# Hybrid encoder on one core: the prompt's attention output goes through DRAM, layer norms stand between output-projection products, w_out's low parts of the sample move to VectorE

## The chip, the cores and the metric

The kernel runs on one core of one Trainium2 chip. It is one program of 20112 instructions. The metric is the device time of one execution in microseconds; the median of three runs before the change is 1564.66 us. TensorE (PE in the profile) multiplies, VectorE (DVE), ScalarE (ACT) and GpSimd (POOL) do the elementwise work, and nearly all DMAs are issued by SyncE (SP), in the order of its queue. Each engine takes its instructions in a fixed order, and an instruction that waits holds up all behind it on its engine.

## The reference

One layer of an encoder runs on two inputs with shared weights: the prompt (512 rows) and the sample (1024 rows), both 1024 wide, all in float32.

```
h = RMSNorm(x); z = h @ w_in                       # 1024 -> 1792: q, k, v, ca, cb
a = windowed attention(q, k, v)                    # 8 heads of 64, 2 kv heads, |q - k| <= 128, bias, sink
c = silu(LayerNorm(dwconv31(ca * sigmoid(cb))))    # 512 channels, norm over channels
x = x + concat(a, c) @ w_out                       # 1024 -> 1024
h = RMSNorm(x); u = dwconv3(h @ w_up)              # 1024 -> 2 x 2816
x = x + (silu(u_gate) * u_value) @ w_down
y = RMSNorm(x)
```

## The kernel before

**Precision.** A float32 product is made of three matmuls on fp32r tiles: each operand is split into a high part, a rounded copy (ScalarE, `split`, L192), and a low part, the difference (L193, on GpSimd, or on VectorE where `dve` is set). So a weight costs one copy, one subtraction and, for a half-product of 128 x 512 with 8 blocks of rows of the weight, 24 matmuls.

**Stages.** The blocks are 128 rows: 0 to 3 are the prompt, 4 to 11 the sample. (1) The prompt's input projection (`proj` and `step`, L299 to L302), 14 chunks of 128 columns. (2) The sample's input projection, the same 14 chunks times two halves of 512 rows, 28 steps; beside it runs the generator `prompt()`: the prompt's attention (`scores`, `values`), its layer norms (`conv_norm`), its output projection (`out_half`, L726 to L728) and its second RMSNorm with transposes (`make_h2`, L776; `transposed`, L258 to L261). (3) The prompt's up-projection, 22 steps of `ffn_step`; beside it, from step 2 on, runs `sample()`: the sample's attention, the loading and splitting of w_out and two of its layer norms. (4) The sample's output projection with the other norms, and then up- and down-projection by products of blocks, up to the end.

**What sets the order.** The program text interleaves the stages by ticks: `proj` calls `tick()` three times in its 24 matmuls and `step` once more, so a step has four. A tick adds `pace["rate"]` to a counter, and for each whole unit the side generator is advanced by one `yield`. The rates are the constants of the head: RB while the prompt's attention runs, RBO from its end on, RD in the up-projection, RN after the sample's attention. In the same way each tick adds a credit for the taps of the 31-wide convolutions, a chain of VectorE instructions (L354), each of which costs 0.66: CA and CB for the prompt's, CL, CLO and CD for the sample's, which are called late. After the main loop of a stage `drain(side)` takes what is left of the side generator, with nothing interleaved. The result is the program order. From it a planner makes the order of each engine: it simulates the engines with costs of its own and lets the earliest instruction of the program go first among those that are ready. `behind` sets an instruction back by a number of places (BACK, for the prompt's and the sample's convolutions).

**Memory.** `sb` hands out fixed slots of SBUF (`h` of 2 KB for each partition, `q` of 4 KB and others); a slot that is used again waits for its last user. The concatenated operand of the output projection is in `cats[i, part]`: part 0 the attention of block i, part 1 the normed convolution, each a high and a low tile. The prompt's part 0 stays in SBUF from `values` to `out_half`; the sample's goes to DRAM (`catd`, L661) and is read back by `load_cat` (L676).

**A layer norm.** `conv_norm` loads the convolution's output from DRAM, transposes it on PE (L690), takes its statistics on VectorE (L692, L693), the power -1/2 on GpSimd (L176, L177), scales on VectorE (L696), yields YN = 2 more times, transposes back on PE (L702), and goes through ScalarE and VectorE to part 1 of `cats` (L705 to L710). For the prompt it first drains the prompt's convolutions.

**An output product.** `out_half(i, n)` makes half n of block i: 24 matmuls with three yields between, and the addition to x (L731). With the second half of a block it stores x, sums its squares (L737) and has the inverse root made on GpSimd. `make_h2` scales the four blocks by it and transposes them; the up-projection's first matmul needs the first transposes of all four.

**A bank.** The up-projection's results lie in two PSUM banks (`u`), which are free again after one ScalarE instruction (L856) and two VectorE instructions (L852) of `up_half`.

Of the kernel before, what the change touches and what calls it, by code (L numbers as in the profile page):

```python
# [36 lines left out]

RA, RB, RBO, RD, RN, RE = 1.2, 0.8, 2.5, 0.8, 0.95, 0.9  # L40


CA, CB = 0.9, 0.4
CL, CLO, CD = 0.6, 1.0, 0.6

NOFF = (4, 7)

SCB, SCD = "aapa", "aaap"


WOP, WOA, DW, DW2 = 1, 5, 2, 0
NE = 2
YN = 2
OB = "uc"
# [2 lines left out]
KEEP = 3  # L57


BACK = (200, 1500)  # L60
U0 = 2


# [82 lines left out]
def tile_hybrid_encoder(ctx: ExitStack, tc: tile.TileContext, xs, rel_bias, norm_attn_g, w_in,  # L146
# [144 lines left out]
    def drain(queue):  # L291
        while queue:
            advance(queue)
# [15 lines left out]
    qsd = [dr.tile([4, P, NH, P], F32, name=f"qsd{i}") for i in range(3)]  # L309
    vsd = dr.tile([P, 2, NKV, 4, P], F32, name="vsd")  # L310
    ksd = dr.tile([HD, NKV, 2, 1024], F32, name="ksd")
    catd = dr.tile([8, P, 2, 4 * P], F32, name="catd")
    cvd = [dr.tile([P, 4, G["T"]], F32, name=f"cvd{G['g']}") for G in GR]
    rs2 = cst.tile([P, 12], F32, name="rs2")

# [303 lines left out]
    def values(u):  # L619
        i, kv = divmod(u, 2)  # L620
        G, b = blocks[i]
        kts = window(i)
        cat = cat_of(i, 0)
        pr = units.pop(u)
        nt0 = 0 if i < 4 else 1
        ht = []

        def turn(n):
            pt = bank("attn")
            for j in range(GRP):  # L630
                nc.tensor.transpose(pt[:, j * P:(j + 1) * P], pr[j][:, 1 + n * P:1 + (n + 1) * P], ident[:])
            hi, lo = sb.tile([NT], F32R), sb.tile([NT], F32R)
            nc.scalar.copy(hi[:], pt[:])
            nc.vector.tensor_tensor(lo[:], pt[:], hi[:].bitcast(F32), op=ALU.subtract)
            ht.append((hi, lo))

        turn(0)
        yield 0.0
        turn(1)
        po = bank("attn")  # L640
        for n, k in enumerate(kts):
            yield 0.0
            hi, lo = ht[n]
            v = vt[nt0 + k // 4][kv][:, k % 4, :]
            nc.tensor.matmul(po[:], v, hi[:], start=(n == 0), stop=False)
            nc.tensor.matmul(po[:], v, lo[:], start=False, stop=(n == len(kts) - 1))
            ht[n] = hi = lo = None
            if n + 2 < len(kts):
                turn(n + 2)
        rows = slice(kv * HD, (kv + 1) * HD)  # L650
        rest = slice((1 - kv) * HD, (2 - kv) * HD)
        c, d = sb.tile([NT]), sb.tile([NT])
        nc.scalar.copy(c[rows, :], po[rest, :])
        nc.scalar.copy(cat[0][rows, :, :], po[rows, :].rearrange("p (j t) -> p j t", t=P))
        nc.vector.tensor_tensor(d[rows, :], po[rows, :], cat[0][rows, :, :].bitcast(F32).rearrange("p j t -> p (j t)"),
                                op=ALU.subtract)
        nc.gpsimd.tensor_tensor(cat[1][rows, :, :].rearrange("p j t -> p (j t)"), d[rows, :], c[rows, :], op=ALU.add)
        if kv == 1 and G["g"] == 1:
            cats.pop((i, 0))
            for L in range(2):  # L660
                nc.sync.dma_start(catd[b, :, L, :].rearrange("p (j t) -> p j t", t=P), cat[L][:].bitcast(F32))  # L661
        yield 0.0

    def attention(u0, u1, then={}):
# [8 lines left out]
    def load_cat(i):  # L673
        cats[i, 0] = (sb.tile([4, P], F32R), sb.tile([4, P], F32R))
        for L in range(2):
            nc.sync.dma_start(cats[i, 0][L][:].bitcast(F32), catd[blocks[i][1], :, L, :].rearrange("p (j t) -> p j t", t=P))  # L676

    def conv_norm(i):
        G, b = blocks[i]
        if G["g"] == 0:  # L680
            drain(convs)
        cat = cat_of(i, 1)
        cv = sb.tile([4, P])
        nc.sync.dma_start(cv[:], cvd[G["g"]][:, :, b * P:(b + 1) * P])
        if G["g"] == 1 and (i, 0) not in cats:
            load_cat(i)
        yield 0.0
        pt = bank("norm")
        for c in range(4):
            nc.tensor.transpose(pt[:, c * P:(c + 1) * P], cv[:, c, :], ident[:])  # L690
        st, mv, rs = sm(6), sm(2), sm(1)
        nc.vector.bn_stats(st[:], pt[:])  # L692
        nc.vector.bn_aggr(mv[:], st[:])  # L693
        rstd_of(mv[:, 1:2], 1.0, rs[:])
        xh = sb.tile([CCH])
        nc.vector.tensor_scalar(xh[:], pt[:], mv[:, 0:1], rs[:], op0=ALU.subtract, op1=ALU.mult)  # L696
        del pt
        for _ in range(YN):
            yield 0.0
        p2 = bank("norm")  # L700
        for c in range(4):
            nc.tensor.transpose(p2[:, c * P:(c + 1) * P], xh[:, c * P:(c + 1) * P], ident[:])  # L702
        y, t = sb.tile([4, P]), sb.tile([4, P])
        for c in range(4):
            nc.scalar.activation(y[:, c, :], p2[:, c * P:(c + 1) * P], AF.Identity,  # L705
                                 scale=lng[:, c:c + 1], bias=lnb[:, c:c + 1])
        nc.scalar.activation(t[:], y[:], AF.Tanh)
        nc.vector.scalar_tensor_tensor(t[:], t[:], 1.0, y[:], op0=ALU.add, op1=ALU.mult)
        nc.scalar.copy(cat[0][:], t[:])
        nc.vector.tensor_tensor(cat[1][:], t[:], cat[0][:].bitcast(F32), op=ALU.subtract)  # L710
        yield 0.0

    xr, x1, wo = {}, {}, {}
    x1d = [dr.tile([P, D], F32, name=f"x1d{i}") for i in range(12)]

    def out_half(i, n):
# [12 lines left out]
            if kc % 2 == 1 and kc < KC - 1:  # L729
                yield 0.0  # L730
        nc.vector.tensor_tensor(x[:, s], po[:], x[:, s], op=ALU.add)  # L731
        if n == 1:
            x1[i] = x
            nc.sync.dma_start(x1d[i][:], x[:])
            ss = sm(1)
# [46 lines left out]

    use.update(step="b", turn="a", attn="au", norm="au", out="u")

    def prompt():
        yield from attention(0, 8, {u: conv_norm(u - 4) for u in range(4, 8)})
        kt.clear(), vt.clear(), qt.clear(), bias.clear()
        pace.update(rate=RBO, late=CLO)
        for n in range(2):
            for kc in range(KC):  # L790
                if (kc, n) not in wor:
                    load_wo(kc, n)
            yield 0.0
            for kc in range(KC):
                split_wo(kc, n, kc % 2 < DW)
                if kc % 2 == 1:
                    yield 0.0
            for i in range(4):
                if n == 0 and i == 3:
                    for kc in range(WOP):  # L800
                        load_wo(kc, 1)
                yield from out_half(i, n)
            wo.clear()
        yield from make_h2(0, 0)

    seq = [(GR[0], j) for j in range(NJ)]
# [105 lines left out]
        want_up(0, half)  # L912
    want_up_raw(1, 0)
    load_bias()
    def sample():
        sink_columns()
        yield from attention(8, 24)
        kt.clear(), vt.clear(), qt.clear(), bias.clear(), score_rows.clear()
        use.update(norm="a")
        pace.update(rate=RN)  # L920
        for m in range(16 + WOA):
            if m in (10, 12):
                load_cat(m // 2 - 1)
            if m < 16:
                load_wo(m // 2, m % 2)
            if m >= WOA:
                split_wo((m - WOA) // 2, m % 2, m % 4 < DW2)
                yield 0.0
        drain(late)
        for m in range(NE):  # L930
            yield from conv_norm(4 + m)

    pace.update(rate=RD, late=CD)
    for k in range(NJ):
# [723 lines left out]
```

## Time and profile before

| | |
|---|---|
| median of 3 runs | 1564.66 us (1561.09 to 1566.85) |
| the profiled execution | 1561.29 us |
| its span, first to last instruction | 1559.5 us |
| mean granted TensorE clock | 0.990 |
| busy: TensorE, VectorE, ScalarE, GpSimd | 1505.8, 1126.9, 795.2, 709.7 us |
| moved between HBM and the core | 227.17 MB, mean 146 GB/s |

Stage 2 lies between about 109 and 366 us, the prompt's up-projection between 366 and 686 us, the sample's output projection between 686 and about 790 us. A row of a stretch of time gives the length of the stretch and then, for each engine in the order PE, PEld (weight loads), DVE, ACT, POOL, its busy time and the number of its instructions; then the granted clock, the DMA engines' busy share and GB/s. A busy PE need not be PE at its peak: matmuls are pipelined, and one of 0.39 us is followed by the next after about 0.23 us. When the clock is at half, that is 0.43 us.

### The profile page before, as it was taken

To read this page: it belongs to the slowest core of one execution; us is meant where nothing else is said; L and a number is where in the kernel's file an instruction comes from. 1 tells how busy PE (TensorE), PEld (TensorE's weight loads), DVE (VectorE), ACT (ScalarE), POOL (GpSimd) and SP (SyncE) were. 2 spreads that over 40 slices of the span, in tenths; PEclk is the share of its full clock that TensorE was granted. 3 is DMA by queue.
4 is the path that set the end of the run, shared out by engine and by line. 5 is a ranking of instruction groups with operands and counts; after the bars stand their busy time and mean duration, and the time that the engine had idled before them with its cause. 6 is when DMAs were issued, how large, how long until landed. Compare 5 with 4: busy or idle time off the path is not lost. (4 is left out here: it accounts for less than half of the span.)

```text
span 1559.5 us, 20112 instructions
## 1 busy us (share of the span) xinstructions
PE 1505.8 (97%) x6843; PEld 1228.9 (79%) x6843; DVE 1126.9 (72%) x1604; ACT 795.2 (51%) x1404; POOL 709.7 (46%) x566
## 2 busy tenths in 40 slices
PE   8998998899999999899999999999999999999997
PEld 6787787787888888777777888888888788888885
DVE  7999767858789785334868777777776845569883
ACT  4634654335787786623455445554545543444354
POOL 6652343226666775947434555555544000003355
PEclk9999999899999999999999999999999999999999
DMA  7582334447344346779332333333332582357644
GB/s 229 157 212 78 108 99 124 128 131 226 111 132 130 117 130 182 241 235 305 108 95 75 102 101 102 102 102 102 102 115 75 191 280 82 105 166 233 220 132 162
DMA packets 228780, 227.17 MB, mean 146 GB/s; under 512 B 13268, under 2 KB 168348, under 8 KB 228549
## 3 DMA queue, kind: packets, MB, share of 16 engines
q1 hardware_dynamic: 228677, 225.88, 45.6%
q8 instruction: 54, 0.88, 0.2%
q14 instruction: 49, 0.40, 0.1%
HBM read 164.74 MB, written 62.14 MB: 145 GB/s over the span
## 5 line engine op out<-in xcount | busy, mean ns | idle before, releaser
L193 POOL TENSOR_TENSOR q<-q,q 128x1024 fp32r<-128x1024 f32 x72 | 173.3, 2414 | 93.5 <-ACT q L192 36.7
L955 POOL TENSOR_TENSOR q<-q,q 128x512 fp32r<-128x512 f32 x101 | 140.7, 1398 | 163.8 <-ACT q L1065 151.5
L955 DVE TENSOR_TENSOR h<-h,h 128x512 fp32r<-128x512 f32 (+2 forms) x202 | 158.4, 817 | 66.2 <-ACT h L959 26.1
L1413 PE MATMUL w<-h,h 128*128 128x512 f32 x462 | 181.4, 393 | 0.5 <-DVE q L1200 0.5
L1414 PE MATMUL w<-h,h 128*128 128x512 f32 x462 | 181.5, 393 | 0.0
L1415 PE MATMUL w<-h,h 128*128 128x512 f32 x462 | 181.1, 392 | 0.0
L1079 PE MATMUL w<-h,q 128*128 128x512 f32 x448 | 176.4, 394 | 3.0 <-ACT w L1171 1.6
L1081 PE MATMUL w<-h,q 128*128 128x512 f32 x448 | 175.5, 392 | 1.0 <-POOL q L955 1.0
L1080 PE MATMUL w<-h,q 128*128 128x512 f32 x426 | 166.5, 391 | 0.0
L299 PE MATMUL u<-h,q 128*128 128x512 f32 x400 | 161.1, 403 | 5.0 <-DVE h L852 4.2
L300 PE MATMUL u<-h,q 128*128 128x512 f32 x400 | 158.9, 398 | 0.0
L302 PE MATMUL u<-h,q 128*128 128x512 f32 x384 | 152.2, 396 | 2.7 <-POOL q L193 2.7
L952 POOL TENSOR_TENSOR q<-q,q 128x1024 f32<-128x1024 f32 x12 | 33.1, 2769 | 238.1 <-DMA h<-gb 197.4
L354 DVE SCALAR_TENSOR_TENSOR c<-c,cvw,c 128x512 f32<-128x512 f32 x184 | 137.9, 750 | 2.9
L959 ACT CAST h<-h 128x512 fp32r<-128x512 f32 x120 | 71.8, 619 | 95.9 <-DVE h L955 42.5
L299 PE MATMUL b<-h,q 128*128 128x512 f32 x256 | 102.3, 400 | 2.7 <-DVE d L384 1.9
L1413 PEld LDWEIGHTS w<-h,h 128*128 128x128 f32 x462 | 86.8, 188 | 20.7 <-ACT h L959 0.9
L1415 PEld LDWEIGHTS w<-h,h 128*128 128x128 f32 x462 | 86.7, 188 | 19.7
L852 DVE SCALAR_TENSOR_TENSOR h<-u,fw,h 128x511 f32<-128x511 f32 x88 | 65.4, 744 | 50.8 <-ACT h L856 50.1
L1414 PEld LDWEIGHTS w<-h,h 128*128 128x128 f32 x462 | 86.8, 188 | 19.4
L1079 PEld LDWEIGHTS w<-h,q 128*128 128x128 f32 x448 | 84.2, 188 | 22.5 <-ACT w L1171 2.1
L302 PE MATMUL b<-h,q 128*128 128x512 f32 x256 | 101.3, 396 | 0.0
(417 smaller groups left out, 3680.3 us busy)
## 6 DMA issues: line engine op xcount, KB each, us to landing
q<-in_w_up SPq DMA_DIRECT2D x88, 512.0 KB
ga<-q SPq DMA_DIRECT2D x64, 256.0 KB
h<-ga SPq DMA_DIRECT2D x57, 256.0 KB
q<-in_w_in SPq DMA_DIRECT2D x28, 512.0 KB
h<-in_w_down SPq DMA_DIRECT2D x52, 256.0 KB
q<-in_x_sample SPq DMA_DIRECT2D x15, 512.0 KB
h<-qsd SPq DMA_DIRECT2D x24, 256.0 KB
x1d<-q SPq DMA_DIRECT2D x11, 512.0 KB
```

Source lines behind the costliest of these rows:

```text
L193: (nc.vector if dve else nc.gpsimd).tensor_tensor(lo[:], raw[:], hi[:].bitcast(F32), op=ALU.subtract)
L299: nc.tensor.matmul(out, whi[:, kc, :], hi[:], start=(kc == 0), stop=False)
L300: nc.tensor.matmul(out, whi[:, kc, :], lo[:], start=False, stop=False)
L302: nc.tensor.matmul(out, wlo[:, kc, :], hi[:], start=False, stop=(kc == KC - 1))
L354: nc.vector.scalar_tensor_tensor(acc[:], src(t), w(t), acc[:], op0=ALU.mult, op1=ALU.add)
L955: (eng or nc.vector).tensor_tensor(out, a, b, op=ALU.subtract)
L1079: nc.tensor.matmul(out, whi[:, s], hi[:], start=(start and c == 0), stop=False, **go)
L1080: nc.tensor.matmul(out, whi[:, s], lo[:], start=False, stop=False, **go)
L1081: nc.tensor.matmul(out, wlo[:, s], hi[:], start=False, stop=(stop and c == 3), **go)
L1413: nc.tensor.matmul(out, sh[:, c], th[:], start=(p == 0), stop=False)
L1414: nc.tensor.matmul(out, sh[:, c], tl[:], start=False, stop=False)
L1415: nc.tensor.matmul(out, sl[:, c], th[:], start=False, stop=(p == NPAIR - 1))
```

## The change

1. *Prompt's attention output through DRAM.* `catd` has 12 blocks instead of 8; `values` stores the prompt's blocks too, and `conv_norm` loads them back.
2. *Order of the prompt's side work.* Norms no longer run inside the attention. After it come norms 0 and 1, the first half of w_out, product (0, 0), then product (1, 0) interleaved with the second half of w_out (`beside`), then (0, 1) and (1, 1), interleaved with norms 2 and 3, then (2, 1), (3, 1), (2, 0), (3, 0), then `make_h2`. `out_half` counts a block's halves instead of taking n = 1 for the last.
3. *The sample's preparation.* `sample()` makes six pieces of w_out's loading and splitting and then interleaves the rest with norms 4 and 5, where it made all pieces first. With DW2 = 4 all low parts of these pieces are made by VectorE; with DW2 = 0 GpSimd made them. The two blocks of attention output are loaded back at pieces 2 and 4 instead of 10 and 12.
4. *Rates.* RB, RBO and RN, the credits CA, CL, CLO and CD, and the sample convolutions' setback change.

```diff
-RA, RB, RBO, RD, RN, RE = 1.2, 0.8, 2.5, 0.8, 0.95, 0.9
+RA, RB, RBO, RD, RN, RE = 1.2, 0.7, 0.6, 0.8, 1.15, 0.9
-CA, CB = 0.9, 0.4
-CL, CLO, CD = 0.6, 1.0, 0.6
+CA, CB = 0.85, 0.4
+CL, CLO, CD = 0.55, 0.9, 0.66
-WOP, WOA, DW, DW2 = 1, 5, 2, 0
+WOP, WOA, DW, DW2 = 1, 5, 2, 4
+WON = 6
-BACK = (200, 1500)
+BACK = (200, 600)
...
-    catd = dr.tile([8, P, 2, 4 * P], F32, name="catd")
+    catd = dr.tile([12, P, 2, 4 * P], F32, name="catd")
...
-        if kv == 1 and G["g"] == 1:
+        if kv == 1:
             cats.pop((i, 0))
             for L in range(2):
-                nc.sync.dma_start(catd[b, :, L, :].rearrange("p (j t) -> p j t", t=P), cat[L][:].bitcast(F32))
+                nc.sync.dma_start(catd[i, :, L, :].rearrange("p (j t) -> p j t", t=P), cat[L][:].bitcast(F32))
...
-        if G["g"] == 1 and (i, 0) not in cats:
+        if (i, 0) not in cats:
             load_cat(i)
...
-        if n == 1:
+        halves_done[i] = halves_done.get(i, 0) + 1
+        if halves_done[i] == 2:
...
+    def beside(gen, other):
+
+        for _ in gen:
+            yield 0.0
+            if next(other, None) is not None:
+                yield 0.0
+        yield from other
+
     def prompt():
-        yield from attention(0, 8, {u: conv_norm(u - 4) for u in range(4, 8)})
+        yield from attention(0, 8)
         kt.clear(), vt.clear(), qt.clear(), bias.clear()
         pace.update(rate=RBO, late=CLO)
-        for n in range(2):
+
+        def w_half(n):
             for kc in range(KC):
                 if (kc, n) not in wor:
                     load_wo(kc, n)
...
-            for i in range(4):
-                if n == 0 and i == 3:
-                    for kc in range(WOP):
-                        load_wo(kc, 1)
+
+        for i in range(2):
+            yield from conv_norm(i)
+        yield from w_half(0)
+        yield from out_half(0, 0)
+        yield from beside(out_half(1, 0), w_half(1))
+        for i, n in ((0, 1), (1, 1)):
+            yield from beside(out_half(i, n), conv_norm(i + 2))
+        for n in (1, 0):
+            for i in (2, 3):
                 yield from out_half(i, n)
-            wo.clear()
+            for kc in range(KC):
+                wo.pop((kc, n))
         yield from make_h2(0, 0)
...
+    def wo_pieces():
+        for m in range(16 + WOA):
+            if m in (2, 4):
+                load_cat(m // 2 + 3)
+            if m < 16:
+                load_wo(m // 2, m % 2)
+            if m >= WOA:
+                split_wo((m - WOA) // 2, m % 2, m % 4 < DW2)
+                yield 0.0
+
+    def norms():
+        drain(late)
+        for m in range(NE):
+            yield from conv_norm(4 + m)
+
     def sample():
         sink_columns()
         yield from attention(8, 24)
...
-        for m in range(16 + WOA):
...
-        drain(late)
-        for m in range(NE):
-            yield from conv_norm(4 + m)
+        wos = wo_pieces()
+        for _ in range(WON):
+            next(wos)
+            yield 0.0
+        yield from beside(wos, norms())
```

More of the change, by code (lines that the diff above doesn't have):

```diff
@@ L675, in load_cat @@
         for L in range(2):
-            nc.sync.dma_start(cats[i, 0][L][:].bitcast(F32), catd[blocks[i][1], :, L, :].rearrange("p (j t) -> p j t", t=P))
+            nc.sync.dma_start(cats[i, 0][L][:].bitcast(F32), catd[i, :, L, :].rearrange("p (j t) -> p j t", t=P))
     def conv_norm(i):
@@ L711, in conv_norm @@
         yield 0.0
-    xr, x1, wo = {}, {}, {}
+    xr, x1, wo, halves_done = {}, {}, {}, {}
     x1d = [dr.tile([P, D], F32, name=f"x1d{i}") for i in range(12)]
@@ L920, in sample @@
         pace.update(rate=RN)
-        for m in range(16 + WOA):
[L922 to L928, printed above, removed]
-        drain(late)
-        for m in range(NE):
-            yield from conv_norm(4 + m)
+        wos = wo_pieces()
[3 more added lines that the diff above has]
+        yield from beside(wos, norms())
     pace.update(rate=RD, late=CD)
```

## Prediction

> **What bounds the kernel now.** I read the page's head first, then the busy time by stretch, then TensorE's own instructions where a stretch falls short, then the other engines at those places.
>
> ```profile
> span 1559.5 us, 20112 instructions
> PE 1505.8 (97%) x6843; PEld 1228.9 (79%) x6843; DVE 1126.9 (72%) x1604; ACT 795.2 (51%) x1404; POOL 709.7 (46%) x566
> ...
> 320.00:360.00 40.00, 40.00 (x180) 32.69 (x179) 26.20 (x36) 14.65 (x24) 10.66 (x14) 1.00 0.52 158
> ...
> 440.00:480.00 40.00, 40.00 (x195) 33.63 (x194) 37.27 (x73) 31.30 (x61) 26.65 (x17) 1.00 0.40 126
> ...
> 640.00:680.00 40.00, 35.83 (x147) 28.48 (x146) 11.77 (x17) 13.95 (x22) 28.93 (x21) 0.91 0.57 183
> ```
>
> TensorE (PE, first number behind the length of a stretch; then weight loads, VectorE, ScalarE, GpSimd, granted clock, DMA share, GB/s) is the bound, and the diff adds no matmul and takes none away. So the change can win only where PE stands idle or runs at a lowered clock, and lose only where it opens new holes. I count the loss of a stretch as its idle time plus busy time times (1 - clock). The stages in question lie between 115 and 690 us. Four holes matter.
>
> Hole 1, the prompt's layer norms between its attention and its output projection:
>
> ```profile
> 265.00:270.00 5.00, 3.27 (x17) 2.51 (x15) 0.88 (x2) 0.72 (x1) 1.73 (x2) 1.00 0.00 0
> 270.00:275.00 5.00, 1.48 (x8) 1.08 (x8) 1.69 (x3) 2.69 (x6) 3.89 (x6) 0.79 0.25 80
> 275.00:280.00 5.00, 2.29 (x7) 1.72 (x8) 3.36 (x5) 2.71 (x6) 0.69 (x3) 0.50 0.67 217
> 280.00:285.00 5.00, 5.00 (x17) 3.95 (x16) 3.30 (x6) 3.92 (x10) 2.43 (x2) 0.69 0.56 193
> ...
> 272.30 0.66 PE L702 MATMUL u<-ident,q 128*128 128x128 f32 x4 [4.03 <-DVE q L696]
> ...
> 276.75 1.08 PE L702 MATMUL u<-ident,h 128*128 128x128 f32 x4 [2.97 <-DVE h L696]
> ```
>
> Idle 20 - 12.04 = 7.96 us, clock 1.48 x 0.21 + 2.29 x 0.50 + 5.00 x 0.31 = 3.0 us: 11.0 us lost. (The two single rows give start, length, engine, line, operation, and in brackets the idle time before it and what ended it.) No engine is full there. It is latency: the second transposes (L702) of a norm wait for the chain statistics, GpSimd power, scaling, and nothing was ordered between them on PE, whose order is fixed. A clean stretch is the one from 320: 180 matmuls, nearly all of 512 columns, in 40 us, 0.22 us each.
>
> Hole 2, the prompt's attention beside the sample's input projection:
>
> ```profile
> 115.00:120.00 5.00, 4.69 (x21) 3.50 (x19) 4.79 (x7) 0.60 (x1) 0.00 (x0) 1.00 0.84 262
> 120.00:125.00 5.00, 2.40 (x14) 2.04 (x15) 4.45 (x15) 1.09 (x4) 0.00 (x0) 1.00 0.43 134
> 150.00:155.00 5.00, 3.93 (x25) 3.12 (x23) 4.47 (x9) 3.81 (x7) 1.88 (x2) 1.00 0.29 80
> 155.00:160.00 5.00, 4.22 (x13) 2.63 (x12) 4.94 (x10) 3.16 (x8) 2.07 (x2) 0.68 0.81 212
> 165.00:170.00 5.00, 3.82 (x23) 2.96 (x22) 4.53 (x9) 4.98 (x12) 1.07 (x1) 1.00 0.02 5
> 170.00:175.00 5.00, 3.50 (x20) 2.63 (x19) 3.78 (x13) 4.88 (x14) 2.83 (x3) 1.00 0.47 139
> ```
>
> 30 - 22.56 = 7.4 us idle and 4.22 x 0.32 = 1.4 us of clock, 8.8 us. VectorE is busy 27 of 30 us here.
>
> Holes 3 and 4, the end of the sample's w_out preparation and the start of its output projection:
>
> ```profile
> 650.00:655.00 5.00, 2.52 (x10) 1.43 (x8) 2.20 (x3) 3.64 (x7) 4.92 (x3) 1.00 0.67 194
> 655.00:660.00 5.00, 3.31 (x8) 2.66 (x9) 2.19 (x3) 0.48 (x1) 5.00 (x4) 0.51 0.58 200
> 660.00:665.00 5.00, 5.00 (x20) 3.93 (x19) 0.00 (x0) 0.05 (x1) 5.00 (x5) 0.80 0.21 81
> 680.00:685.00 5.00, 4.67 (x25) 3.72 (x23) 0.29 (x1) 1.10 (x3) 0.00 (x0) 1.00 1.08 368
> 685.00:690.00 5.00, 3.14 (x15) 2.59 (x16) 4.31 (x7) 3.60 (x8) 4.36 (x5) 1.00 1.06 376
> ...
> 656.69 0.76 PE L299 MATMUL u<-h,q 128*128 128x512 f32 x1 [3.50 <-DVE h L852]
> ...
> 651.30 7.00 POOL L193 TENSOR_TENSOR q<-q,q 128x1024 fp32r<-128x1024 f32 x3
> 658.26 7.50 POOL L193 TENSOR_TENSOR h<-h,h 128x512 fp32r<-128x512 f32 x6
> ...
> 652.64 0.62 ACT L192 CAST h<-h 128x512 fp32r<-128x512 f32 x1 [1.36 <-DMA h<-in_w_out]
> ...
> 654.21 0.77 ACT L856 ACTIVATE h<-u,vecs,fw 128x512 f32<-128x512 f32 x1
> ```
>
> Hole 3 is 2.48 + 1.69 idle and 3.31 x 0.49 + 5.00 x 0.20 = 2.6 of clock: 6.8 us. Hole 4 is 0.33 + 1.86 = 2.2 us. In hole 3 GpSimd is full with w_out's low parts in between w_up's, and the release of a PSUM bank (L856 on ScalarE, then L852 on VectorE) comes late because L856 is queued behind copies of w_out of which one waits for its DMA.
>
> **The change part by part.** *Norms of prompt.* The number of instructions is the same. The side work is advanced by ticks, four for each of the sample's 28 projection steps, 112 in all. Before, attention and norms are 68 advances at 0.8 (85 ticks), and the other 50 go at 2.5 and end near tick 106, inside the projection. After, attention is 52 advances at 0.7 and so ends at tick 75 or 76; 36 ticks at 0.6 give 22 more: norms 0 and 1 (8), the first half of w_out (5), product (0,0) (4), and a little over half of the 9 that product (1,0) shares with the second half. So the first two norms have projections around them, about 10 matmuls or 2.2 us for each advance and three advances between L690 and L702, against a stall of 4.03 us; norms 2 and 3 have 12 matmuls of a product between the two transposes, 12 x 0.22 = 2.6 us, which leaves up to 1.4 us of stall each. I take 2.5 us as what is left of hole 1: gain **8.5** (bounds 0, if the planner lays it out as before, and 11).
>
> *What is late next.* Six and a half half-products come after the sample's last projection. They cover the norms, but nothing covers the step behind them: make_h2 needs block 3's row sums, and the up-projection needs make_h2. Before, projections lay there: PE is busy 40.00 of 40 us from 320 to 360. The chain, as it ran then:
>
> ```profile
> 353.85 0.69 DVE L731 TENSOR_TENSOR q<-u,q 128x512 f32<-128x512 f32 x1 [0.83 <-PE u L728]
> ...
> 354.57 1.06 ACT L737 ACTIVATE h<-q 128x1024 bf16<-128x1024 f32 x1 [1.52 <-DVE q L731]
> ...
> 356.69 0.75 DVE L776 TENSOR_SCALAR q<-q,rs 128x1024 f32<-128x1024 f32 x1
> ...
> 364.71 1.83 ACT L260 ACTIVATE h<-a,vecs 128x512 fp32r<-128x512 f32 x3
> ...
> 376.74 0.50 PE L302 MATMUL u<-h,q 128*128 128x512 f32 x1 [1.50 <-POOL q L193]
> ```
>
> From 353.85 to 357.44 is 3.6 us; transposes and the first copy (1.83 / 3 = 0.6) make it about 4.8, the low part on VectorE some 0.8 more, and the clock falls as in hole 3 (2.6). That is 8 us; the sample's first score products can fill about 1.5. New loss **6.5** (bounds 2, if the planner keeps projections back, and 10, if convolution taps stand inside the chain). The 1.5 us wait for w_up's low part at 376.74 should vanish, since GpSimd gets to it during the tail: gain **1.5** (0 to 1.5).
>
> *Attention.* Without the norms in it, the forced end of the prompt's convolutions moves from tick 44 to tick 76, and 0.7 for 0.8 takes an eighth off the attention's load on VectorE for each tick. Its start (2.9 us lost by 125) stays. Of the rest, 5.9 us, I take a third: gain **2** (-4 to +6, as the order of every instruction here is new).
>
> *Through DRAM.* Eight more stores and eight more loads of 256 KB:
>
> ```profile
> L661 SPq DMA_DIRECT2D catd<-h x16: 319/320/532, 431.5 to 651.6; - x16
> ...
> SPq L661 <- ACT h L654: 25.1, 6, 5.8
> ```
>
> 16 issues at 0.32 us are about 5.1 us on SP's queue, and the stores add waits there (25.1 us in six for the sample's 16, so some 13, the longest 5.8). Behind them stand the loads of w_in, which go out two chunks ahead; a chunk is 48 matmuls, 10.6 us. So 5.8 is hidden: **0** (bounds -2 and 0; with that lead gone, one wait of 5.8).
>
> *Low parts of w_out.*
>
> ```profile
> L193 POOL TENSOR_TENSOR h<-h,h x16: 1267/1292/1309, 630.1 to 666.3; 128x512 fp32r<-128x512 f32 x16
> L193 DVE TENSOR_TENSOR h<-h,h x12: 675/691/693, 224.3 to 322.1; 128x512 fp32r<-128x512 f32 x12
> ...
> L852 DVE SCALAR_TENSOR_TENSOR h<-u,fw,h 128x511 f32<-128x511 f32 x88 | 65.4, 744 | 50.8 <-ACT h L856 50.1
> ```
>
> 16 x 1.29 = 20.6 us leave GpSimd, 16 x 0.69 = 11.0 us come to VectorE, which has 28 of 40 us free from 640 on. The late sample convolutions move a little later (0.55 and 0.66 for 0.6, and a setback of 600 for 1500 places); from 440 VectorE is at 37.27 of 40 and PE still loses nothing, so I give this 0. GpSimd's part of hole 3 goes; ScalarE's 16 copies and the DMA behind 652.64 stay. Gain **4.5** (0 to 6.8). A bank must be free within a half-product, 24 x 0.22 = 5.3 us, of which L856 and two L852 take 0.77 + 1.49 = 2.3: VectorE may be 3.0 us late before PE sees it.
>
> One row speaks against it:
>
> ```profile
> 293.36 1.45 DVE L193 TENSOR_TENSOR q<-h,h 128x512 fp32r<-128x512 f32 x1
> ...
> 291.60 2.66 POOL L193 TENSOR_TENSOR q<-q,q 128x1024 fp32r<-128x1024 f32 x1 [0.16 <-ACT q L192]
> ```
>
> The same low part took 1.45 us while GpSimd ran one. At that price the 16 are 23.2 us and not 11.0. The Trainium skill ("GPSIMD Engine Reference", Specifications) says that GpSimd shares its SBUF interfaces with VectorE and that the two contend where a VectorE instruction has two SBUF inputs; this low part has two, and the trace agrees.
>
> *Norms of sample.* Interleaved with w_out from the seventh piece on and at 1.15, they are 24 advances in 21 ticks where it was 25, so that norms 4 and 5 end before the up-projection does. Hole 4: gain **1.5** (-1 to 2.2).
>
> Sum: 8.5 - 6.5 + 1.5 + 2 + 0 + 4.5 + 1.5 = 11.5 us. The profiled execution took 1561.3 us (span 1559.5 and 1.8 around it), so 1549.8; the median of the runs shown, 1564.7, is 3.4 above it, so **1553 us**. All lower bounds taken together give 1582, all upper ones 1539.
>
> **Rivals.** *The hole only moves* (no change): the gain of hole 1 is paid back by make_h2 at 8 to 10 us, attention gives nothing, and hole 3 stays, since ScalarE's wait for the DMA caused it. For it: L856 stood behind that copy, which the diff does not touch. Against it: GpSimd full for 15 us in hole 3. 8.5 - 9 + 1.5 + 1 = 2: 1563 us.
>
> *Contention.* Low parts at 1.45 us: two of them in front of an L852, one held by a copy's DMA wait of 1.36, are 4.3 us, over the 3.0 of slack, so hole 3 stays though GpSimd is free. Against it: with 20.6 us gone GpSimd is no longer busy all the time. 1553 + 4.5: 1557.5 us. This is what the Trainium skill's rule would bring about.
>
> *The bare tail* (slower): once projections have run out, each wait of the output projection is PE's. Both halves of w_out are now resident at once, 32 tiles where it was 16, so slots for the second half come late. If norms 2 and 3 stall as before, hole 1 gains nothing; make_h2 costs 10, and the second half keeps PE waiting as long as the longest wait above, 5.8, with 2.6 of clock behind it: 18.4 us against 9.5 of other gains, 8.9 slower, 1573.6 us. It decides from 9.5 us of bare waits on. Against it: the products stand between the norms' transposes, and the loads have free SP time.
>
> **Chances.** Forecast 0.58, own range 1543 to 1560; only moved 0.18; contention 0.08; bare tail 0.16. A measurement here tells about 0.5% (7.8 us) from no change: faster means under 1556.8, slower over 1572.5. Of the forecast 0.52 is below the first bound, 0.06 within; contention 0.01 and 0.07; moved 0.16 within and 0.02 slower; tail 0.01 and 0.15. Faster 0.53, same 0.30, slower 0.17. The range goes from the sum of the upper bounds, 1539, to 1574, the nearer half of the bare tail.
>
> **What would show it.** Right: PE's stretch of the prompt's norms with L702 waiting under 1.5 us; one new wait of 4 to 6 us at the first L258 or L299 of the prompt's up-projection, waiting for L776 or L260, with the clock near 0.5 behind it; GpSimd's L193 with no 128x512 form, VectorE's 16 more, of 0.7 to 1.45 us; no 3.5 us wait for L852. Wrong: L702 waiting 3 us and more, PE waiting for w_out in the tail, VectorE near full with new waits for L852 between 400 and 640, or a larger loss in the attention.

## The result, and the profile after

The change makes the kernel slightly slower: 1570.08 us median (1566.72 to 1575.37, 11 runs) against 1561.09 us (1557.86 to 1566.85, 11 runs) of the kernel before on the same chip, ratio **1.0052** with a 95% interval of 1.0039 to 1.0065. The forecast was 1553 us and faster; the time is inside the range, on the wrong side. The changed file has one constant line more in its head, so L193 of before is L194 of after, L702 is L703, L726 is L727, L776 is L778; from `sample()` on the shift is larger (L852 is L870, L856 is L874, L1002 is L1029).

Head of the page of the kernel after:

```profile
span 1568.1 us, 20157 instructions
PE 1509.4 (96%) x6843; PEld 1232.7 (79%) x6843; DVE 1147.1 (73%) x1620; ACT 795.3 (51%) x1404; POOL 694.5 (44%) x550
```

As many matmuls as before, VectorE 20 us busier, GpSimd 15 us less. So the 8.6 us between the spans are idle time and lowered clock of TensorE. Busy time by stretch, columns as in the prediction:

```profile
265.00:270.00 5.00, 5.00 (x25) 4.10 (x24) 2.31 (x5) 3.14 (x8) 3.20 (x4) 1.00 0.70 195
270.00:275.00 5.00, 5.00 (x24) 4.11 (x23) 3.08 (x3) 2.46 (x5) 4.76 (x4) 1.00 0.74 235
275.00:280.00 5.00, 5.00 (x24) 4.14 (x23) 4.91 (x7) 4.46 (x10) 1.86 (x2) 1.00 0.97 348
280.00:285.00 5.00, 5.00 (x23) 3.93 (x21) 3.58 (x6) 1.61 (x3) 0.00 (x0) 1.00 0.27 102
...
355.00:360.00 5.00, 0.55 (x3) 0.31 (x3) 1.92 (x3) 1.15 (x2) 4.20 (x5) 0.83 0.29 115
360.00:365.00 5.00, 3.51 (x11) 2.61 (x12) 4.75 (x8) 2.95 (x5) 0.29 (x1) 0.50 0.50 157
375.00:380.00 5.00, 2.97 (x15) 2.30 (x13) 4.15 (x6) 3.29 (x4) 3.50 (x3) 1.00 0.66 177
380.00:385.00 5.00, 2.61 (x6) 2.16 (x7) 5.00 (x12) 2.30 (x5) 3.92 (x2) 0.72 0.51 138
...
655.00:660.00 5.00, 4.25 (x19) 3.23 (x18) 4.80 (x6) 1.54 (x3) 5.00 (x3) 1.00 0.95 290
660.00:665.00 5.00, 3.79 (x17) 2.80 (x17) 4.71 (x7) 1.11 (x3) 1.31 (x3) 1.00 0.79 270
...
705.00:710.00 5.00, 4.01 (x21) 3.05 (x19) 0.00 (x0) 0.00 (x0) 3.71 (x7) 1.00 0.91 303
710.00:715.00 5.00, 0.44 (x2) 0.20 (x2) 2.08 (x3) 0.62 (x1) 2.99 (x5) 0.83 1.05 378
715.00:720.00 5.00, 1.96 (x8) 1.43 (x8) 1.32 (x2) 2.13 (x5) 3.48 (x6) 0.50 0.95 286
720.00:725.00 5.00, 3.78 (x10) 2.82 (x9) 2.66 (x4) 0.62 (x1) 3.43 (x6) 0.50 0.96 313
```

Hole 1 is gone: full rows from 265 to 285, where 7.96 us were idle. Of hole 3 about 2 us are left from 655 to 665, with VectorE now full where GpSimd was. There are two new holes, one before and in the start of the prompt's up-projection (355 to 385) and one in the sample's output projection (705 to 725), where nothing had been expected. The stretch from 700 to 760 as a whole, first before and then after (length, TensorE's busy time and instructions, clock, DMA share, GB/s):

```profile
700.00:760.00 60.00, 57.01 (x269) 1.00 0.78 263
```

```profile
700.00:760.00 60.00, 46.55 (x196) 0.86 0.77 247
```

What TensorE waited for in the two new holes:

```profile
355.80 0.55 PE L259 MATMUL a<-ident,q 128*128 128x128 f32 x3 [1.06 <-DVE q L778]
361.13 0.90 PE L259 MATMUL a<-ident,q 128*128 128x128 f32 x3 [4.79 <-DVE q L778]
...
382.39 0.77 PE L300 MATMUL u<-h,q 128*128 128x512 f32 x1 [4.42 <-DVE h L870]
...
712.54 0.44 PE L1029 MATMUL b<-ident,q 128*128 128x128 f32 x2 [3.53 <-DVE q L1000]
716.17 1.09 PE L703 MATMUL a<-ident,h 128*128 128x128 f32 x4 [3.19 <-DVE h L697]
719.13 1.09 PE L691 MATMUL a<-ident,h 128*128 128x128 f32 x4 [1.88 <-DMA h<-cvd]
```

To set stages against each other I use one measure for all runs: the time between the starts of successive matmul groups of the timeline, less what their matmuls take back to back (0.229 us for 512 columns, 384 and 256 in proportion, about 0.087 us for a transposition of 128). It holds idle time and lowered clock alike. Over the span it gives 86.0 us before and 95.3 after, so 9.3 of difference for 8.6 between the spans. By stretch, in us:

| kernel | ratio (interval) | 100-180 | 180-340 | 340-400 | 620-700 | 700-760 | all |
|---|---|---|---|---|---|---|---|
| before | | 12.2 | 15.9 | 3.0 | 10.9 | 5.5 | 86.0 |
| after | 1.0052 (1.0039-1.0065) | 13.0 | 4.3 | 15.7 | 4.4 | 20.5 | 95.3 |
| prompt's part alone | 1.0045 (1.0031-1.0058) | 11.6 | 2.6 | 15.8 | 15.5 | 6.3 | 91.7 |
| sample's part alone | 1.0018 (1.0001-1.0036) | 14.9 | 6.2 | 2.7 | 5.4 | 19.5 | 89.1 |
| after, slots rotated | 0.9999 (0.9981-1.0017) | 11.7 | 5.4 | 16.5 | 4.3 | 11.4 | 87.9 |
| sample's part, slots rotated | 0.9935 (0.9913-0.9957) | 12.2 | 6.4 | 4.0 | 6.1 | 12.2 | 77.3 |
| after, norm of block 6 early | 1.0011 (1.0001-1.0021) | 11.8 | 5.4 | 17.1 | 9.6 | 5.4 | 91.0 |

The stretches are read from one profile each. The two sample's-part kernels have the same order of instructions up to 670 us and differ by 2.7 us from 100 to 180; less than 3 us in one stretch is not read as an effect.

### The profile page after: what moved, and what is told of

It reads as the page before. It is cut to its first block, busy times and chain, and to the rows that moved or that the text cites. A ratio compares the mean times of both kernels' runs of the same rounds, so it can differ in the third digit from the quotient of the medians.

```text
span 1568.1 us, 20157 instructions
## 1 busy us (share of the span) xinstructions
PE 1509.4 (96%) x6843; PEld 1232.7 (79%) x6843; DVE 1147.1 (73%) x1620; ACT 795.3 (51%) x1404; POOL 694.5 (44%) x550
## 5 line engine op out<-in xcount | busy, mean ns | idle before, releaser
L194 POOL TENSOR_TENSOR q<-q,q 128x1024 fp32r<-128x1024 f32 x72 | 174.1, 2424 | 100.8 <-ACT q L193 50.9
L300 PE MATMUL b<-h,q 128*128 128x512 f32 x256 | 103.2, 403 | 3.3 <-DVE d L385 2.0
L193 ACT CAST q<-q 128x1024 fp32r<-128x1024 f32 x72 | 75.6, 1051 | 59.1 <-DMA q<-in_w_in 26.4
L303 PE MATMUL b<-h,q 128*128 128x512 f32 x256 | 102.1, 399 | 0.0
L301 PE MATMUL b<-h,q 128*128 128x512 f32 x256 | 102.1, 399 | 0.0
```

The lines of the kernel that those rows point to most:

```text
L194: (nc.vector if dve else nc.gpsimd).tensor_tensor(lo[:], raw[:], hi[:].bitcast(F32), op=ALU.subtract)
L300: nc.tensor.matmul(out, whi[:, kc, :], hi[:], start=(kc == 0), stop=False)
L301: nc.tensor.matmul(out, whi[:, kc, :], lo[:], start=False, stop=False)
L303: nc.tensor.matmul(out, wlo[:, kc, :], hi[:], start=False, stop=(kc == KC - 1))
```

## Experiments

**Which half loses.** First the changed kernel with everything of `sample()` and its constants as before; then the reverse.

```diff
-RA, RB, RBO, RD, RN, RE = 1.2, 0.7, 0.6, 0.8, 1.15, 0.9
+RA, RB, RBO, RD, RN, RE = 1.2, 0.7, 0.6, 0.8, 0.95, 0.9
-CL, CLO, CD = 0.55, 0.9, 0.66
+CL, CLO, CD = 0.6, 0.9, 0.6
-WOP, WOA, DW, DW2 = 1, 5, 2, 4
+WOP, WOA, DW, DW2 = 1, 5, 2, 0
-BACK = (200, 600)
+BACK = (200, 1500)
...
-        wos = wo_pieces()
-        for _ in range(WON):
-            next(wos)
-            yield 0.0
-        yield from beside(wos, norms())
```

The second kernel is the one before with these same constants and the new `wo_pieces`, `norms` and `sample` as in the changed one, and its prompt untouched.

> The prompt's part of the change alone (round trip, norms between the products, its rates), the sample's part as before. Theory: the hole of the prompt's norms is mended (11 us), the bare step behind the last half-product costs about 8 us and the late PSUM bank after it about 5, and the sample's output projection has no hole of over 4 us: 0 to 4 us slower than before. Rival (the planner lays out everything anew, the place of the edit does not matter): a hole of 8 us or more in the sample's output projection here too, 8 us slower or more.

> The sample's part alone (w_out's low parts on VectorE, norms 4 and 5 interleaved, its rates and the late convolutions'), the prompt's part as before. Theory: the hole around 655 us shrinks by 4 to 5 us, and the output projection gets a hole of 10 us or more at the norm of block 6, whose load waits for a slot that the last gate's tile holds: 3 to 9 us slower than before. Rival (the prompt's part is to blame for both): no hole at block 6, 4 us faster than before.

Measured: 1.0045, 7 us slower, and 1.0018, 3 us slower, so both halves lose. The table shows where: the prompt's part mends hole 1 (15.9 to 2.6) and opens the tail (3.0 to 15.8); the sample's part mends holes 3 and 4 (10.9 to 5.4) and opens the hole at 700 (5.5 to 19.5). The prompt's part alone loses more than the 0 to 4 us that were expected, as 620 to 700 gets 4.6 us worse with it (10.9 to 15.5); no run gives the cause of that. The sample's part also mends hole 1, though it leaves the prompt's norms where they were (15.9 to 6.2); this comes up again below.

**The hole at 700: an inherited slot.** The norm of block 6 loads its conv tile in this stretch. The SP queue of before and of after, and the GpSimd row that writes the last gate tile in after (rows: start, length, engine, line, operation):

```profile
684.10 0.54 SPq L684 DMA_DIRECT2D h<-cvd  x1
```

```profile
691.46 1.30 POOL L900 TENSOR_TENSOR h<-h,h 128x512 f32<-128x512 f32 x1
...
694.53 0.50 SPq L901 DMA_DIRECT2D gt<-h  x1
...
700.88 0.56 SPq L685 DMA_DIRECT2D h<-cvd  x1
```

The load goes out 16.8 us later. Its tile got the SBUF slot that the last gate tile had held; that tile is stored at 694.53, after GpSimd made it behind a run of pair sums (L911 to L914, sums and differences of two gate tiles). The planner counts with this, and puts the load and the norm behind it later. The test adds and removes no instruction: at the norm of block 6 the four free slots at the head of the list go to its end. The order is the same up to that place, about 680 us; after it 123 of 6843 places differ on TensorE, 60 of 841 on SP, 47 of 550 on GpSimd, the last of them at 755 us.

```diff
 def conv_norm(i):
+    if i == 6:
+        for s in [s for s in sb.free if s[0][0] == "h"][:4]:
+            sb.free.remove(s)
+            sb.free.append(s)
```

> The changed kernel, with no instruction changed; only the four oldest free slots are put at the end of the list when the norm of block 6 begins, so that its tiles do not take those of the last gate product. Theory: the load of block 6's convolution goes out before 690 us where it was 700.9, and most of the 14 us hole between 708 and 744 us goes: 7 to 12 us faster than the changed kernel, 2 us faster or the same as before. Rival (the hole comes from GpSimd's queue, where the pair sums stand in front of the power, or from the low parts): within 2 us of the changed kernel.

Measured 0.9999 against before, some 8 us faster than after. The load and what is left of the hole, after with slots rotated:

```profile
685.37 0.56 SPq L689 DMA_DIRECT2D h<-cvd  x1
...
723.41 0.55 POOL L178 TENSOR_TENSOR s<-s,nhalf 128x1 f32<-128x1 f32 x1
...
732.94 0.80 PE L731 MATMUL c<-h,h 128*128 128x512 f32 x1 [5.09 <-ACT h L714]
```

From 700 to 760 the loss falls from 20.5 to 11.4. One wait of 5.09 us stays, for the next norm: its statistics were ready at 716.85, but its power (L178) stood among GpSimd's pair sums and came at 723.41. That is read from the rows; no run moves the pair sums. The same rotation on the sample's part alone gives a kernel that beats both:

> The sample's part alone, with the four oldest free slots put at the end of the list when the norm of block 6 begins. Theory (slots): the hole between 700 and 740 us falls from 18 to 10 us or less, 7 to 10 us faster than the sample's part alone, 3 to 7 us faster than before. Rival (the early norms 4 and 5 themselves starve the output projection): within 3 us of the sample's part alone.

Measured 0.9935 (0.9913 to 0.9957), median 1555.52 us, 13 us faster than the sample's part alone where 7 to 10 was expected; 700 to 760 falls by 7.3 (19.5 to 12.2), as expected. A second way to the same end leaves the slots alone and puts block 6's norm before the output projection:

```diff
-NE = 2
+NE = 3
```

> The changed kernel with three of the sample's norms in the up-projection instead of two (NE = 3): block 6's norm stands before the sample's output projection, so its conv load asks for a slot before the last gate tiles do. Theory slot: the hole from 701 to 725 us, which began with block 6's conv load behind the last gate tile, goes; 700 to 760 loses 6 to 12 us instead of 20.5, ratio 0.996 to 1.000, unless the three norms bare the end of the up-projection. Rival: the power of the norms behind GpSimd's pair sums makes the hole whatever slot the load has; then 700 to 760 stays above 17 us and the ratio at 1.005.

> The fastest version so far (the sample's part alone with rotated slots, 0.9935) with three norms of the sample in the up-projection instead of two. It still loses 12.2 us from 700 to 760, with waits for norms 6 and 7. Theory slot: nothing to win from the slot here, since it is rotated already; what is left are the powers of norms behind pair sums, of which one fewer is then left in that stretch: 2 to 4 us faster, 0.991 to 0.992. Rival: the third norm bares the end of the up-projection as hole 4 did before, 2 us slower, 0.995.

On the changed kernel 700 to 760 falls from 20.5 to 5.4, the ratio from 1.0052 to 1.0011. That is not quite the 1.000 or less that was expected; part is given back from 620 to 700 (4.4 to 9.6), where the third norm now stands. So the hole hangs on when block 6's norm can start, whichever way it is moved. On the rotated sample's part it is 0.9937 (0.9916 to 0.9959): 4.5 us less from 700 to 760, 3.1 more from 760 to 860, no gain that can be told.

**The tail.** The chain after the last product, in the kernel after, in the timeline:

```profile
355.66 0.68 DVE L732 TENSOR_TENSOR q<-u,q 128x512 f32<-128x512 f32 x1
...
356.37 1.06 ACT L739 ACTIVATE h<-q 128x1024 bf16<-128x1024 f32 x1 [4.22 <-DVE q L732]
...
355.82 2.35 POOL L194 TENSOR_TENSOR q<-q,q 128x1024 fp32r<-128x1024 f32 x1 [0.63 <-DVE q L778]
358.13 1.26 POOL L348 TENSOR_TENSOR h<-h,h 128x512 f32<-128x512 f32 x1
359.47 0.19 POOL L177 TENSOR_SCALAR rs<-s 128x1 f32<-128x1 f32 x1
...
360.33 0.75 DVE L778 TENSOR_SCALAR q<-q,rs 128x1024 f32<-128x1024 f32 x1 [0.21 <-POOL rs L178]
...
377.76 1.04 ACT L193 CAST q<-q 128x1024 fp32r<-128x1024 f32 x1 [0.85 <-PE u L303]
378.71 1.44 ACT L874 ACTIVATE h<-u,vecs,fw 128x512 f32<-128x512 f32 x2
```

The row sums end at 357.53, and the inverse root (L177) starts at 359.47: a low part of w_up and a piece of convolution stand in front of it on GpSimd, 2 us. Then, 20 us on, the second cost: the transposes of h2 trickle in, both half-products of the first up step advance side by side and end together (377.3), so both banks are full at once and wait for L874, which stands behind a copy of w_up (377.76), and for L870 on VectorE: 4.42 us. Two tests. One covers the tail: all four norms behind the attention, products in the order of before, the rates of the prompt's side work raised until projections are left over.

```diff
-RA, RB, RBO, RD, RN, RE = 1.2, 0.7, 0.6, 0.8, 1.15, 0.9
+RA, RB, RBO, RD, RN, RE = 1.2, 0.8, 1.6, 0.8, 1.15, 0.9
...
+        for i in range(4):
+            yield from conv_norm(i)
+        for n in range(2):
...
+            for i in range(4):
+                if n == 0 and i == 3:
+                    for kc in range(WOP):
+                        load_wo(kc, 1)
                 yield from out_half(i, n)
```

> The changed kernel with all four norms of the prompt behind its attention, the products in the order of before and the rates 0.8 and 1.6, so that the sample's projection lasts until the second RMSNorm is made. Theory: the wait of 4.8 us for the scaling and the 4.4 us for the bank go, the norms stay covered, the sample's hole stays: 8 to 13 us faster than the changed kernel, 0 to 4 us faster than before. Rival (it is the load of VectorE in the tail that costs, not the missing cover): within 3 us of the changed kernel.

Measured 1.0218 (1.0198 to 1.0238). The tail does go (15.7 to 3.7), but 180 to 340 loses 31.0 us where it was 4.3. There TensorE waits 5.8 us in three pieces for VectorE to empty a bank of the projection, 5.2 for a conv load and 4.5 for copies and low parts of w_out. The kernel is 26 us slower than after, where 8 to 13 us faster was expected: this order covers the tail at a price far above it. The other test takes only the bank wait away, by letting the first up step use the other pair of banks (slots rotated in both):

```diff
+    use.update(up="ub")
     for k in range(NJ):
...
         ffn_step(k)
+        use.update(up="u")
```

> The changed kernel with rotated slots, and the first step of the prompt's up-projection writes to two banks of another group (b), so that its second step finds the banks u free. Theory: the wait of 4.4 us for a bank at the start of the up-projection, which came because both half-products of the first step ended together, goes with the clock behind it: 4 to 6 us faster than with rotated slots alone. Rival (the wait only moves to the low parts of w_up, whose loads are late too): within 2 us of it.

Measured 1.0012 (0.9996 to 1.0028), no gain against 0.9999. The tail falls from 16.5 to 9.5 as expected, so the bank wait was worth 7 us with what follows it; and from 620 to 700 the loss rises from 4.3 to 11.6. Why is the next point.

**Low parts of w_out on VectorE.** The largest group of L194 in the kernel after on GpSimd and on VectorE (shortest, median, longest in ns):

```profile
L194 POOL TENSOR_TENSOR q<-q,q x72: 2346/2406/2850, 15.9 to 657.8; 128x1024 fp32r<-128x1024 f32 x72
...
L194 DVE TENSOR_TENSOR h<-h,h x24: 661/683/2823, 272.9 to 678.8; 128x512 fp32r<-128x512 f32 x24
```

The move alone, in the kernel before:

```diff
-WOP, WOA, DW, DW2 = 1, 5, 2, 0
+WOP, WOA, DW, DW2 = 1, 5, 2, 4
```

> The kernel of before with the low parts of the sample's w_out on VectorE and nothing else. By the prediction's term: hole 3 falls from 6.8 to about 2 us, 4.5 us faster. Rival (ScalarE's copies and their DMA make the hole): within 2 us of before. Rival (contention with GpSimd): the low parts take 1 us and more each, and waits for the bank stay.

Measured 1.0008 (0.9993 to 1.0023), no change. From 620 to 700 it loses 9.1 us instead of 10.9, too little to be read, and from 700 to 860 it loses 7 us more, for which there is no test. Hole 3 stands, and what comes last there is now VectorE:

```profile
647.45 7.97 DVE L193 TENSOR_TENSOR h<-h,h 128x512 fp32r<-128x512 f32 x4
...
656.18 1.53 DVE L852 SCALAR_TENSOR_TENSOR h<-u,fw,h 128x511 f32<-128x511 f32 x2
...
647.69 0.65 PE L299 MATMUL u<-h,q 128*128 128x512 f32 x1 [1.94 <-DVE h L852]
...
657.86 0.60 PE L299 MATMUL u<-h,q 128*128 128x512 f32 x1 [2.36 <-DVE h L852]
```

Four low parts take 7.97 us, 2.0 each and not 0.68, and the two L852 that free the bank come behind them. The kernel with the other banks shows it at its worst (first VectorE, then GpSimd at the same time, then TensorE):

```profile
643.94 5.68 DVE L194 TENSOR_TENSOR h<-h,h 128x512 fp32r<-128x512 f32 x2 [1.47 <-POOL h L904]
...
643.86 7.97 POOL L194 TENSOR_TENSOR q<-q,q 128x1024 fp32r<-128x1024 f32 x3
...
655.71 0.77 PE L300 MATMUL u<-h,q 128*128 128x512 f32 x1 [5.30 <-DVE h L874]
```

Two low parts take 5.68 us while GpSimd runs three of its own back to back. Taken singly, each of the two ends 0.55 us after the GpSimd low part beside it (646.81 after 646.26, 649.62 after 649.07). One can be held by two GpSimd instructions in a row: in the same kernel a low part lasts from 636.86 to 640.41, 3.56 us, while GpSimd is busy without a gap from 635.82 to 639.87. The Trainium skill ("SBUF — State Buffer", section "SBUF: two separate sides") says that a VectorE instruction with two SBUF inputs and a GpSimd instruction that reads SBUF lock each other out, the one that starts first keeping the shared ports for its whole length and the other being blocked. The trace agrees, by these times. The same two kernels with these low parts on GpSimd again (DW2 = 0):

> The sample's part alone with rotated slots (ratio 0.9935 before), but with w_out's low parts on GpSimd as in the kernel before (DW2 = 0). Theory of the prediction: low parts on VectorE gain 4.5 us, so this is 4.5 us slower than the version with DW2 = 4: ratio 0.9965, the wait for L852's counterpart near 650 longer than 3 us. Theory contention: on VectorE the fourteen low parts from 600 to 700 us took 15.8 us instead of 14 x 0.69 = 9.7 where GpSimd ran its own low parts at the same time, single ones 2.1 to 2.8 us, so that nothing was won: ratio 0.9935 within 0.002.

> The changed kernel with rotated slots and with the first up-projection step in the other pair of banks, but w_out's low parts of the sample on GpSimd (DW2 = 0). With them on VectorE this version lost 1.4 + 8.1 us in two places: the tail had got 7 us better, and hole 3 had come back, 9.5 us from 640 to 660, where TensorE waited 5.3 us for VectorE's second L874 behind low parts of 2.84 us each. Theory contention: the low parts on VectorE, stretched from 0.68 to 2.8 us by GpSimd's own low parts, make that wait; on GpSimd they leave VectorE alone, the wait for L874 near 650 falls under 2 us, and the kernel is 4 to 6 us faster than that version: ratio 0.997. Rival: ScalarE, held 6 us by a copy of w_out that waits for its DMA, sets the bank's release; then hole 3 stays at 7 us or more and the ratio is 1.001.

The rotated sample's part: 0.9935 (0.9915 to 0.9955), as with them on VectorE. (The 15.8 us of the recorded text are those of all 16 low parts in that stretch, not of fourteen, so 15.8 for 11.0.) The version with the other banks: 1.0003 (0.9988 to 1.0018) against 1.0012, not to be told apart. Its wait near 650 falls from 5.30 to 2.36 us, not under 2, and the loss from 620 to 700 does not fall (11.6 and 12.8, of which 2.55 are a wait for a conv load). This is what the rival said. Now ScalarE is late (L878 is L874 of after in these files):

```profile
644.85 1.35 ACT L193 CAST h<-h 128x512 fp32r<-128x512 f32 x2 [2.41 <-DMA h<-in_w_out]
648.75 1.05 ACT L193 CAST q<-q 128x1024 fp32r<-128x1024 f32 x1 [2.55 <-DMA q<-in_w_up]
...
653.15 0.78 ACT L878 ACTIVATE h<-u,vecs,fw 128x512 f32<-128x512 f32 x1
```

So two things can hold this bank, VectorE's stretched low parts and ScalarE's copies behind their DMA, and taking one away leaves the other. What the sample's part gains in holes 3 and 4 does not come from where the low parts are made (6.1 and 7.7 us left with VectorE and with GpSimd, 10.9 before). It comes with the rest of that part: norms 4 and 5 interleaved with w_out, the rate RN and the credit CD, which no run takes apart.

**Hole 1 and one constant.** The sample's part alone had mended hole 1. Of its constants only CL acts there: the kernel with CL alone has the same order on every engine up to 377 us. The setback, 600 for 1500 places, leaves the order of every engine as it was.

```diff
-CL, CLO, CD = 0.6, 1.0, 0.6
+CL, CLO, CD = 0.55, 1.0, 0.6
```

> The kernel before with one constant of the change alone: the credit CL for the sample's late convolution taps while the prompt's attention runs, 0.55 for 0.6. (The setback BACK, 600 for 1500, changes the place of no instruction on any engine, so it needs no run.) In the run with the sample's part alone the prompt's norms are ordered as before, and yet hole 1 was gone: 0.6 us lost from 260 to 280 us where it was 10.5. Theory A: hole 1 is an accident of where the planner put the projections around the norms, and this constant alone closes it: L702's waits of 4.0 and 3.0 us vanish, about 10 us faster, ratio 0.993 to 0.994, the rest as before. Theory B: hole 1 closed there because of something else in the sample's part; then L702 still waits and the ratio is 1.000.

Measured 0.9964 (0.9950 to 0.9978). From 180 to 340 the loss is 6.0 instead of 15.9, and no L702 waits (a bracket would show idle time):

```profile
279.82 0.60 PE L702 MATMUL u<-ident,q 128*128 128x128 f32 x4
...
287.00 0.60 PE L702 MATMUL u<-ident,h 128*128 128x128 f32 x4
```

Theory A holds for the place; some of it is given back from 100 to 180 (16.8) and from 700 to 760 (8.3), so that the whole is 0.36% and not 0.65%.

**The round trip.** Alone, in the order of before:

```diff
-    catd = dr.tile([8, P, 2, 4 * P], F32, name="catd")
+    catd = dr.tile([12, P, 2, 4 * P], F32, name="catd")
-        if kv == 1 and G["g"] == 1:
+        if kv == 1:
-        if G["g"] == 1 and (i, 0) not in cats:
+        if (i, 0) not in cats:
```

> The kernel of before with the prompt's attention output stored to DRAM and loaded again by the norm, and nothing else. By the prediction's term: 0 to 2 us slower. Rival (the load stands behind the store, and the norm's tiles change slots): a new wait of 3 us and more at the prompt's output projection, 4 us slower or more.

Measured 1.0168 (1.0136 to 1.0200), 26 us slower. Waits of the SP queue from 195 to 225 us in this kernel, its load for the first norm, and that norm on TensorE:

```profile
SPq L661 <- ACT h L654: 9.7, 1, 9.7
...
223.55 0.58 SPq L684 DMA_DIRECT2D h<-cvd  x1
...
232.53 1.12 PE L702 MATMUL a<-ident,h 128*128 128x128 f32 x4 [4.53 <-DVE h L696]
```

In the kernel before that load goes out at 194.75. Here a store that waits 9.7 us for the attention's output stands ahead of it in the queue, and a load of w_in that waits for its slot; the norm comes 29 us later, with no projections around it. The loss is 18.8 us from 100 to 180 and 29.2 from 180 to 340. The queue's waits are not all of it: the planner's order on TensorE is another from about 134 us on, and this run does not tell the cost of the waits (16.0 us in four for these stores up to 235 us) from that of the new order. In the changed order the same trip was then taken out of the changed kernel:

> The changed kernel with the prompt's attention output kept in SBUF as before (catd of 8 blocks, no store and no load for blocks 0 to 3), all else as in the changed kernel. In the order of the kernel before, the round trip alone cost 26 us: its stores stand in the SP queue waiting for the attention's output (12.0 us in two waits), and behind them the loads of the conv blocks and of w_in. Theory A: in the changed order too the stores hold the queue; then the loss between 100 and 180 us falls from 13.0 by 2 to 6 us, and the kernel is 2 to 6 us faster than the changed one: ratio 1.001 to 1.004. Theory B: with the norms behind the attention nothing that matters stands behind the stores, so the trip costs nothing there: loss between 100 and 340 us the same within 2 us, ratio 1.005. The hole near 705 us, which hangs on which SBUF slot a tile gets, may come out differently in either case and is read apart.

Measured 1.0065 (1.0044 to 1.0085), not faster than after (1.0052). The loss is 11.7 and 4.3 us in these two stretches, 13.0 and 4.3 with the trip. So theory B: what the trip costs depends on the order that it stands in. With norms inside the attention it is 26 us, with the norms behind it nothing that can be told. That this is for what stands behind its stores in the queue fits the rows and is not shown by itself.

## Why the prediction was wrong

The steps of its sum against the loss by stretch:

| step | forecast | measured |
|---|---|---|
| hole 1 | +8.5 | +11.6 |
| make_h2, and the wait for w_up's low part | -6.5 + 1.5 | -12.7 |
| attention | +2 | -0.8 |
| through DRAM | 0 | 0 (13.0 and 4.3 with it, 11.7 and 4.3 without) |
| holes 3 and 4 | +4.5 + 1.5 | +6.5 |
| the sample's output projection | no term | -15.0 |
| all the rest | 0 | +1.1 |
| sum | +11.5 faster | 9.3 slower |

**The step that failed** is the sentence that "the stages in question lie between 115 and 690 us". With it the sum has no term for new holes behind 690 us, though the same paragraph says that the change loses where it opens new holes. It left out the stage right behind, whose first norm takes its slot from a pool that the changed `sample()` hands out in another order. Block 6's conv load inherited the slot of the last gate tile and went out 16.8 us late, and from 700 to 760 the kernel loses 15.0 us more than before. Rotating the slots takes back 9.1 of it, moving the norm early all of it, with 5.2 lost elsewhere; what rotating leaves is mostly the wait of 5.09 us for the next norm. With those 9.1 us back the kernel is level with the one before (0.9999). No rival had it either.

**The second, a size:** the tail. The wait was where it was forecast, on L259 for L778, 4.79 us with the clock at 0.50 behind it. Two things were missing from the 6.5 us: GpSimd's two instructions in front of the inverse root (2 us, read from the rows and not tested; the forecast had given the chain GpSimd as free), and the bank wait of 4.42 us that follows when both half-products of the first up step end together (7 us with what follows it, by the test with the other banks). With 1.5 us that were to be won there, 5.0 were forecast and 12.7 came. The bare tail, the rival on the slower side at 1573.6 us, was near the time, but not for its reasons: norms 2 and 3 did not stall and w_out was not late.

**Right:** hole 1 closed as described, and nothing of the products' interleaving failed. But the reordering was not needed for it: a credit of 0.55 closes it as well. The hole was an accident of the order of before, and a forecast that credits its end to one edit can't tell that another edit of the same change would do it too.

**Right in size, wrong in cause:** holes 3 and 4. The forecast gave 4.5 us to the low parts' move at 0.69 us each, 11.0 for 16. In the kernel after, the 16 took 16.6 us (VectorE's busy time on L194 from 600 to 700 us), the longest 2.82; alone the move gains nothing, and with it undone the gain stays. The contention rival had the mechanism, and its price of 1.45 us was too low: in the one row that it was read from, the subtraction started at 293.36, when GpSimd's instruction (291.60, 2.66 us long) had only 0.90 us left, and ended 0.55 us after it. When the two start together, as at 643.9 above, the wait covers GpSimd's whole instruction of 2.4 us, and the subtraction takes 2.87. The other cause of hole 3 is the one that the first rival named, L856 behind a copy that waits for its DMA.

**Right, by luck of the place:** the round trip at 0. The reason given, that w_in's loads have a lead, does not hold by itself: in the order of before the trip costs 26 us, with a store's wait of 9.7 us in front of those loads, far over the 2 us that were its bound and over the one wait of 5.8 without the lead.

## What to carry to other kernels

When a program is ordered by a planner and its tiles take turns in fixed slots, an edit can change the order and the slots of everything behind it: list the loads that stand next after the edited stage, see which tile each slot had before, and ask when that one is done. Before a gain is credited to an edit, change the smallest constant near it alone; a stall that two unrelated edits each close is no measure of either. Work that is moved from one busy engine to another should be priced with the other still running, from the row where the two start together, not from the shortest or from one that overlaps by chance.

## What had not been expected of the hardware

A VectorE subtraction of 128 x 512 with both inputs in SBUF took 0.68 us alone and up to 2.82 us in the kernel after beside GpSimd's two-input subtractions (3.56 us in the kernel with the other banks, behind two GpSimd instructions in a row). GpSimd's own rose from 2.4 to at most 2.84 us: the three of this row of the kernel after, which run while those of VectorE are stretched, took 2.72, 2.84 and 2.39 us.

```profile
652.35 7.88 POOL L194 TENSOR_TENSOR q<-q,q 128x1024 fp32r<-128x1024 f32 x3
```

So of the two, VectorE pays most: in one kernel 5.68 us for two instructions that take 1.37 us alone.
